# Conformer convolution and RWKV-7 block: the convolution's running sum moved from SBUF to PSUM, and the chain's four products put into one PSUM bank

## The chip, the core and the metric

The kernel runs on one core of a Trainium2 chip. Five engines share the work, each with its own queue of instructions that it takes strictly in order: PE (TensorE, matrix products; its weight loads are shown as PEld), DVE (VectorE), ACT (ScalarE), POOL (GpSimd) and SP (SyncE, which here only issues transfers). The metric is the device time of one execution in microseconds (us), with the three runs given beside it.

## What is computed

One decoder block, over 2048 tokens of 1024 channels, in float32. The parts that the change touches are the depthwise convolution and the RWKV-7 scan:

```
h = rmsnorm(x, norm_g) * (1 + scale) + shift          # adaLN from c
p = h @ w_in                                           # all branches in one projection
u = val * sigmoid(gate)
u = causal depthwise conv of u, 31 taps per channel, + conv_b
y_conv = (silu(layernorm(u)) * silu(og)) @ w_conv_out
per head, per token:                                   # 16 heads of 64
    sk    = state @ kk
    state = state * w - sk b^T + v k^T
    o     = state @ r
y_rwkv = (groupnorm(o) + bonus) * silu(r_og) @ w_rwkv_out
out = rmsnorm(x + gate * ((sigmoid(g_conv) y_conv + sigmoid(g_rwkv) y_rwkv) @ w_out), final_g)
```

## The kernel before, in words

**Tiling.** The 2048 tokens go through in 4 blocks of 512 (`TB`). Channels lie on the 128 partitions, so a tile is 128 channels by 512 tokens; 1024 channels make 8 such tiles (`KT`). Every projection is `mm3`: the float32 operands are split into a high and a low part, and three products (high-high, low-high, high-low) sum up in one PSUM tile `ps_main`. That is line 173, in the first stage 48 products of 256 columns for one tile of output.

**Two stages.** The first stage walks the 4 blocks; in each it walks 4 groups of 4 heads (`group`). Between the steps of a group it hands out `fill` work: `conv` for two channel tiles and `gates` for eight projections. Its end is at about 2690 us. The second stage (layer norm, output projections, final norm) follows; the change touches nothing in it.

**One group.** (1) `pair`, for two pairs of heads: projections, decay, and the products `As` of line 504 to 506. (2) The triangular systems of 32 by 32 are written to DRAM and read back with one system on each partition (`La`). POOL then solves them: 31 steps of a product `itmp` (line 568) and a sum `TT` (line 570), each step needing the one before. All inputs and outputs of both are in SBUF. (3) `TT` goes through DRAM back into `As`; DVE transposes 32 by 32 pieces of it (`T`, line 591), PE joins the halves (lines 597 and 606). (4) The chain: 8 chunks of 64 tokens, one after the other. In each, PE multiplies the state `S` and the older values (lines 624 and 629) into `xo`; DVE copies the half `x` of it to SBUF (`X`, line 632); PE applies the solved system (line 637); DVE scales the solution into `uv` (line 639); PE makes the state increment (line 643); DVE adds it to the state in four instructions (line 648); PE adds the solution's part to the output half `o` of `xo` (line 654), and ACT copies `o` out (line 656).

**The convolution.** `conv` makes `u` (512 tokens and 30 of the block before), and DVE sums the 31 taps: one TENSOR_SCALAR that makes `yj` (line 714) and 30 SCALAR_TENSOR_TENSOR, each `yj = u[shifted] * ck + yj` (line 717). There are 4 blocks of 8 tiles, so 960 of the latter.

**PSUM.** It has 8 banks of 2 KB per partition, and a tile takes whole banks here: `pm` 2 (`ps_main`), `pl` 1 (`late`), `px` 2 (`xo`), `pg` 1 (`gd`), `pa` 2 (`aux`). `gd` holds a chunk's solution and its state increment.

**What sets the order.** Each engine's order is written when the program is built: a scheduler places the instructions by their dependencies, its own durations and a few priorities. What another engine or a transfer must have finished is a semaphore wait in front of an instruction, and whatever is behind it in that engine's queue waits too. Accesses of two engines to one PSUM bank of one tile are kept apart by such waits, even where they touch different columns.

Of the kernel before, what the change touches and what calls it, by code (L numbers as in the profile page):

```python
# [9 lines left out]
F32 = mybir.dt.float32  # L10
# [3 lines left out]
ALU = mybir.AluOpType  # L14
AX = mybir.AxisListType
PSUM = bass.MemoryType.PSUM
DRAM = bass.MemoryType.DRAM

P = 128
D = 1024  # L20
KT = D // P
TB = 512
NTT = TB // P
# [3 lines left out]
HALO = CONVW - 1  # L27
# [55 lines left out]
def hybrid_block(ctx: ExitStack, tc: tile.TileContext, x, vecs, convk, w2a2, final_g, ada, w_in, w_co, w_ro, w_o, crow, out,  # L83
                 seq=2048, groups=(0, 1, 2, 3), phase2=True, dbg=None):
    nc = tc.nc
# [24 lines left out]
    def vc(name, j=None):  # L110
        o, w = VOFF[name]
        return v[:, o:o + w] if j is None else v[:, o + j:o + j + 1]
# [105 lines left out]
    lt = late.enter_context(tc.tile_pool(name="lt", bufs=2))  # L218
    pl = late.enter_context(tc.tile_pool(name="pl", bufs=1, space=PSUM))
    px = late.enter_context(tc.tile_pool(name="px", bufs=PXB, space=PSUM))  # L220
    pg = late.enter_context(tc.tile_pool(name="pg", bufs=1, space=PSUM))
    e1 = early.enter_context(tc.tile_pool(name="e1", bufs=1, side="right"))
    xp = early.enter_context(tc.tile_pool(name="xp", bufs=HXB, side="right"))
    hp = early.enter_context(tc.tile_pool(name="hp", bufs=1, side="right"))
# [117 lines left out]
    def hprep0(xs, ada_steps):  # L342
# [16 lines left out]
        wf_ = {}  # L359
        for k in range(KT):  # L360
            next(ada_steps)
            pt = (pl, pg)[k % 2].tile([P, NTT, P], F32, name="ps_x", tag=("late", "gd")[k % 2])
            for tt in range(NTT):
                nc.tensor.matmul(pt[:, tt, :], xs[tt][:, k * P:(k + 1) * P], dg[:, tt, :], start=(tt == 0),
                                 stop=(tt == NTT - 1), skip_group_check=True)
            hf = hx("hf0")
            nc.scalar.activation(hf, flat(pt), AF.Identity, scale=g_col[:, k:k + 1], bias=shift_col[:, k:k + 1])
            hsplit(h, k, hf)
            for i, ti in enumerate(tiles_):
                if k == i // 2:  # L370
                    hl = None
                    if i >= 2:
                        hl = [l3.tile([P, KT, P], F32R, name="w_f", tag="tk", bufs=TKB) for _ in range(4 - i)]
                        if i == 3:
                            hl.append(lt.tile([P, KT, P], F32R, name="w_f", tag="La", bufs=1))
                    wf_[ti] = load_w("in", ti, hl)
                    front[ti] = (pm, px)[i // 2].tile([P, TB], F32, name="ps_f", tag=("main", "xo")[i // 2])

            for i, ti in enumerate(tiles_):
                if ti in wf_ and k > i // 2:  # L380
                    for kk in range(0 if k == i // 2 + 1 else k - 1, k):
                        mm3k(front[ti], wf_[ti], h, kk)
# [152 lines left out]
    def group(b, g, h, lora, fill):  # L535
# [79 lines left out]
        for c in range(NCH):  # L615
# [3 lines left out]
            Se = lt.tile([P, 2, P], F32, name="Se", tag="Se", bufs=1)  # L619
            for q in range(2):  # L620
                nc.scalar.mul(Se[:, q, :], Sg[:, q, :], R[q]["pe"][:, c:c + 1])
            xo = px.tile([P, 2, P], F32, name="xo", tag="xo")
            for q in range(2):
                nc.tensor.matmul(xo[:, q, :], R[q]["KR"][:, cc, es], Sg[:, q, :], start=(q == 0), stop=False,
                                 skip_group_check=True)
# [3 lines left out]
                    nc.tensor.matmul(xo[pr_, q, hs], As[q][vr, hh, c, kcol(e)], uv[vr, c, q, hs],  # L629
                                     start=False, stop=False, skip_group_check=True)  # L630
            X = lt.tile([P, 2, P], F32, name="X", tag="X", bufs=1)
            nc.vector.tensor_copy(X[pr_], xo[pr_])  # L632
            gd = pg.tile([P, 4, P], F32, name="gd", tag="gd")
            for q in range(2):
                for hh in range(2):
                    hs = slice(64 * hh, 64 * hh + 64)
                    nc.tensor.matmul(gd[pr_, q, hs], As[q][pr_, hh, c, kcol(e)], X[pr_, q, hs],  # L637
                                     start=(q == 0 and hh == 0), stop=(q == 1 and hh == 1), skip_group_check=True)
            nc.vector.tensor_tensor(out=uv[pr_, c].rearrange("p q (h n) -> p q h n", n=64),
                                    in0=gd[pr_, 0:2].rearrange("p q (h n) -> p q h n", n=64),  # L640
                                    in1=rn[pr_, :, cc, :].unsqueeze(3).broadcast_to([64, 2, 2, 64]), op=ALU.mult)
            for q in range(2):
                nc.tensor.matmul(gd[:, 2 + q, :], R[q]["tk"][:, c, :], uv[:, c, q, :], start=(q == 0), stop=(q == 1),  # L643
                                 skip_group_check=True)
            for q in range(2):
                for hh in range(2):
                    hs = slice(64 * hh, 64 * hh + 64)
                    nc.vector.scalar_tensor_tensor(out=Sg[hs, q, hs], in0=gd[hs, 2 + q, hs],  # L648
                                                   scalar=R[q]["pe"][hs, c:c + 1], in1=Se[hs, q, hs],
                                                   op0=ALU.mult, op1=ALU.add)  # L650
            for q in range(2):
                for hh in range(2):
                    hs = slice(64 * hh, 64 * hh + 64)
                    nc.tensor.matmul(xo[vr, q, hs], As[q][:, hh, c, rcol(e)], uv[:, c, q, hs],  # L654
                                     start=False, stop=(q == 1 and hh == 1), skip_group_check=True)
            nc.scalar.copy(O[vr, cc], xo[vr])  # L656


        O16 = O.rearrange("p a q (h n) -> p a (q h) n", n=64)
# [43 lines left out]
    def conv(b, h, j):  # L703
# [6 lines left out]
        with tc.high_priority(HP):  # L710
            nc.vector.scalar_tensor_tensor(out=u[:, HALO:], in0=th, scalar=1.0, in1=pvl, op0=ALU.add, op1=ALU.mult)
        nc.gpsimd.tensor_copy(tail[:, j, :], u[:, TB:])
        yj = e2.tile([P, TB], F32, name="yj", tag="yj", bufs=1)
        nc.vector.tensor_scalar(out=yj, in0=u[:, HALO:], scalar1=ck[:, j, HALO:HALO + 1], scalar2=vc("conv_b", j),
                                op0=ALU.mult, op1=ALU.add)
        for i in range(HALO):
            nc.vector.scalar_tensor_tensor(out=yj, in0=u[:, i:i + TB], scalar=ck[:, j, i:i + 1], in1=yj,  # L717
                                           op0=ALU.mult, op1=ALU.add)
        nc.sync.dma_start(y_dram[b][j], yj)

    def gates(b, h, j, which="1234"):
# [368 lines left out]
```

## Time and profile before

| | |
|---|---|
| median of 3 runs | 3379.35 us (3379.3 to 3392.31) |
| the profiled execution, its own time | 3373.04 us |
| its span, first to last instruction | 3371.3 us |
| mean granted clock of TensorE | 0.959 |
| busy: PE, DVE, ACT, POOL | 3110.2, 2378.0, 1063.8, 1587.6 us |
| the 960 taps on DVE (line 717) | 802.3 us |
| the solve on POOL (lines 568 and 570) | 274.2 and 279.5 us |

The profile is of one execution. A view by groups has the line, the engine, the operation, output<-inputs by the program's names, shapes and the count; behind the bar the busy time in us and the mean ns of one; behind the second bar the idle time of the engine just before them, and what ended it. A view by stretches has, for each stretch of the span in us, the busy time of each engine with the number of its instructions, the granted clock of TensorE, and the share and rate of the transfers. Some products (those of line 624, for one) are recorded twice in the profile and stand once in the order.

### The profile page before, as it was taken

What the parts mean: (1) busy time and instruction counts of PE and PEld (TensorE: products, weight loads), DVE (VectorE), ACT (ScalarE), POOL (GpSimd) and SP (SyncE); (2) the same over time, 40 slices, a digit from 0 to 9 for tenths busy, and PEclk for the clock granted to TensorE, in tenths of its full rate; (3) what the DMA queues carried; (4) which work ended last, traced back from release to release, by engine and by line L of the source; (5) the groups of instructions that cost most, each with busy time, mean ns of one, the idle gap of its engine ahead of it and who ended that gap; (6) DMA issues with size and microseconds to landing.
All of it is one profiled execution on the core that took longest, in us unless ns stands there. A gap on an engine that the chain in (4) does not pass through costs nothing.

```text
span 3371.3 us, 65315 instructions
## 1 busy us (share of the span) xinstructions
PE 3110.2 (92%) x25664; PEld 2874.4 (85%) x25664; DVE 2378.0 (71%) x4712; ACT 1063.8 (32%) x1900; POOL 1587.6 (47%) x2158
## 2 busy tenths in 40 slices
PE   6889898999999989999999899999989898878998
PEld 5789898888899988898989898989989877667887
DVE  7786777776677665767666567757688656889755
ACT  4432433332223131323232314132322223344422
POOL 3375454534544535253636355727576413746201
PEclk9999999999999999899999999999999999898999
DMA  7765656663546465445554556646446655655543
GB/s 295 243 210 181 230 174 222 222 197 119 177 142 190 140 184 166 148 132 174 159 155 150 182 165 215 211 124 186 158 127 200 217 181 188 216 184 177 179 158 124
DMA packets 328468, 606.98 MB, mean 180 GB/s; under 512 B 130848, under 2 KB 147552, under 8 KB 328160
## 3 DMA queue, kind: packets, MB, share of 16 engines
q1 hardware_dynamic: 265088, 373.14, 33.7%
q0 software_dynamic: 63072, 229.67, 22.0%
q8 instruction: 202, 3.31, 0.4%
q14 instruction: 106, 0.87, 0.1%
HBM read 439.03 MB, written 162.53 MB: 178 GB/s over the span
## 4 chain that ended last, share of the span: by engine, by line
PE 46%; DVE 18%; POOL 15%; DMA 11%; issue 6%; SPq 2%; ACT 2%; POOLq 0%; DVEq 0%; ACTq 0%
PE ps_main L173 30%; POOL TT L570 5%; POOL itmp L568 5%; DVE yj L717 5%; PE aux L504 3%; DMA As<-dT 2%; DMA dT<-TT 2%; DMA La<-dA 1%; PE gd L637 1%; PE xo L654 1%; PE xo L629 1%; DMA dA<-As 1%; POOL w_lo L158 1%; PE gd L643 1%; PE pout L1007 1%
## 5 line engine op out<-in xcount | busy, mean ns | idle before, releaser
L173 PE MATMUL ps_main<-h_hi,w_hi 128*128 128x256 f32 x4608 | 981.0, 290 | 39.8 <-DVE th L700 18.0
L173 PE MATMUL ps_main<-h_hi,w_lo 128*128 128x256 f32 x4608 | 973.5, 289 | 26.4 <-POOL w_lo L158 24.4
L173 PE MATMUL ps_main<-h_lo,w_hi 128*128 128x256 f32 x4608 | 964.9, 288 | 0.2 <-DVE h_lo L328 0.2
L717 DVE SCALAR_TENSOR_TENSOR yj<-u,ck,yj 128x512 f32<-128x512 f32 x960 | 802.3, 836 | 21.8
L173 PEld LDWEIGHTS ps_main<-h_hi,w_hi 128*128 128x128 f32 x4608 | 732.0, 193 | 60.4 <-issue 21.5
L173 PEld LDWEIGHTS ps_main<-h_hi,w_lo 128*128 128x128 f32 x4608 | 730.7, 193 | 40.5 <-POOL w_lo L158 27.0
L173 PEld LDWEIGHTS ps_main<-h_lo,w_hi 128*128 128x128 f32 x4608 | 730.1, 193 | 8.2 <-issue 1.2
L568 POOL TENSOR_TENSOR itmp<-La,TT 128x126 f32<-128x126 f32 (+22 forms) x496 | 274.2, 553 | 105.1 <-DMA La<-dA 73.5
L156 ACT CAST w_hi<-w_st 128x1024 fp32r<-128x1024 f32 x167 | 175.5, 1051 | 446.5 <-DMA w_st<-w_in_t 114.7
L570 POOL TENSOR_TENSOR TT<-TT,itmp 128x126 f32<-128x126 f32 (+22 forms) x496 | 279.5, 564 | 32.7
L149 POOL DMA_DIRECT2D w_hi<-kh_in x219 | 126.8, 579 | 348.5 <-PE ps_main L173 323.9
L158 DVE TENSOR_TENSOR w_lo<-w_st,w_hi 128x1024 fp32r<-128x1024 f32 x120 | 162.9, 1357 | 132.8 <-PE ps_main L173 50.3
L648 DVE SCALAR_TENSOR_TENSOR S<-gd,pe,Se 64x64 f32<-64x64 f32 x512 | 144.7, 283 | 91.6 <-PE gd L643 82.6
L158 POOL TENSOR_TENSOR w_lo<-w_st,w_hi 128x1024 fp32r<-128x1024 f32 x47 | 117.8, 2506 | 94.8 <-ACT w_hi L156 91.2
L656 ACT COPY uv<-xo 64x256 f32<-64x256 f32 x128 | 47.1, 368 | 342.6 <-PE xo L654 270.4
L506 DVE TENSOR_TENSOR As<-aux,maskA 128x512 f32<-128x512 f32 x128 | 88.3, 691 | 86.1 <-PE aux L504 85.8
L1018 POOL TENSOR_TENSOR xt<-xt,tg 128x256 f32<-128x256 f32 x60 | 52.8, 901 | 199.2 <-DVE tg L1014 192.0
L522 POOL TENSOR_TENSOR vv<-rk,vv 128x512 f32<-128x512 f32 x32 | 45.2, 1412 | 210.6 <-PE aux L519 152.5
L504 PE MATMUL aux<-KR,BKz 128*128 128x128 f32 x1024 | 138.2, 279 | 3.1 <-ACT rk L492 2.3
L504 PEld LDWEIGHTS aux<-KR,BKz 128*128 128x128 f32 x1024 | 125.2, 191 | 7.3 <-ACT rk L492 2.8
L591 DVE STREAM_TRANSPOSE T<-As 32x32 f32<-32x32 f32 x512 | 58.0, 166 | 102.7 <-DMA As<-dT 101.5
L632 DVE COPY X<-xo 64x256 f32<-64x256 f32 x128 | 53.7, 420 | 102.8 <-PE xo L629 101.5
(293 smaller groups left out, 5867.1 us busy)
## 6 DMA issues: line engine op xcount, KB each, us to landing
w_hi<-kh_in POOLq DMA_DIRECT2D x219, 512.0 KB, 4.0
w_lo<-kl_in POOLq DMA_DIRECT2D x219, 512.0 KB, 5.1
w_st<-w_in_t SPq DMA_DIRECT2D x73, 512.0 KB, 4.6
kh_in<-w_hi SPq DMA_DIRECT2D x71, 512.0 KB, 3.1
kl_in<-w_lo SPq DMA_DIRECT2D x71, 512.0 KB, 3.9
w_st<-w_ro_t SPq DMA_DIRECT2D x32, 512.0 KB, 4.0
w_st<-w_co_t SPq DMA_DIRECT2D x32, 512.0 KB, 3.8
w_st<-w_o_t SPq DMA_DIRECT2D x32, 512.0 KB, 3.6
```

What stands on the lines that cost most here:

```text
L149: nc.gpsimd.dma_start(hi, back[0])
L156: nc.scalar.copy(hi, st)
L158: lo_eng.tensor_tensor(out=lo, in0=st, in1=hi.bitcast(F32), op=ALU.subtract)
L173: nc.tensor.matmul(ps[:, qs], ww[:, k, :], aa[k][:, qs], start=(k == 0 and t == 0 and q == 0), stop=(k == KT - 1 and t == 2 and q == ms - ...
L504: nc.tensor.matmul(pA[:, c // 2, es], BKz[:, hh, cc, es], KR[:, cc, es], start=(c == 0), stop=(c == 3), skip_group_check=True)
L506: nc.vector.tensor_tensor(out=Asb[:, hh, c4 * 4:c4 * 4 + 4, :].rearrange("p (a e) n -> p a (e n)", e=2), in0=pA, in1=flat(maskA).unsqueeze ...
L568: nc.gpsimd.tensor_tensor(out=tmp[:, :ni, :nt], in0=La[:, j:j + 1, j + 1:].broadcast_to([P, ni, nt]), in1=TT[:, :ni, j:j + 1].broadcast_to ...
L570: nc.gpsimd.tensor_tensor(out=TT[:, :ni, j + 1:], in0=TT[:, :ni, j + 1:], in1=tmp[:, :ni, :nt], op=ALU.add)
L591: nc.vector.transpose(T11[lo_, q, hh, c, :], As[q][lo_, hh, 2 * c + e, lo_])
L632: nc.vector.tensor_copy(X[pr_], xo[pr_])
L648: nc.vector.scalar_tensor_tensor(out=Sg[hs, q, hs], in0=gd[hs, 2 + q, hs], scalar=R[q]["pe"][hs, c:c + 1], in1=Se[hs, q, hs], op0=ALU.mult ...
L717: nc.vector.scalar_tensor_tensor(out=yj, in0=u[:, i:i + TB], scalar=ck[:, j, i:i + 1], in1=yj, op0=ALU.mult, op1=ALU.add)
```

## The change

Three edits, which belong together because PSUM has no ninth bank.

1. The taps. The running sum is a PSUM tile `acc` (pool `pc`, one bank). The first instruction and 29 of the 30 taps write `acc`; the last tap reads `acc` and writes `yj` in SBUF, from where it is stored as before.
2. The chain. `gd` and its pool are gone. `xo` has four parts of 128 columns instead of two: the solution goes over `x` in the first two, the state increment into the other two. Its first product no longer begins an accumulation of its own, since the bank was begun by the chunk's first product.
3. `hprep0`, which used the banks of `late` and `gd` in turn before the first block, uses those of `late` and `acc`.

```diff
--- before.py
+++ after.py
@@ -218,7 +218,7 @@
     lt = late.enter_context(tc.tile_pool(name="lt", bufs=2))
     pl = late.enter_context(tc.tile_pool(name="pl", bufs=1, space=PSUM))
     px = late.enter_context(tc.tile_pool(name="px", bufs=PXB, space=PSUM))
-    pg = late.enter_context(tc.tile_pool(name="pg", bufs=1, space=PSUM))
+    pc = late.enter_context(tc.tile_pool(name="pc", bufs=1, space=PSUM))
     e1 = early.enter_context(tc.tile_pool(name="e1", bufs=1, side="right"))
     xp = early.enter_context(tc.tile_pool(name="xp", bufs=HXB, side="right"))
     hp = early.enter_context(tc.tile_pool(name="hp", bufs=1, side="right"))
@@ -359,7 +359,7 @@
         wf_ = {}
         for k in range(KT):
             next(ada_steps)
-            pt = (pl, pg)[k % 2].tile([P, NTT, P], F32, name="ps_x", tag=("late", "gd")[k % 2])
+            pt = (pl, pc)[k % 2].tile([P, NTT, P], F32, name="ps_x", tag=("late", "acc")[k % 2])
             for tt in range(NTT):
                 nc.tensor.matmul(pt[:, tt, :], xs[tt][:, k * P:(k + 1) * P], dg[:, tt, :], start=(tt == 0),
                                  stop=(tt == NTT - 1), skip_group_check=True)
@@ -619,7 +619,9 @@
             Se = lt.tile([P, 2, P], F32, name="Se", tag="Se", bufs=1)
             for q in range(2):
                 nc.scalar.mul(Se[:, q, :], Sg[:, q, :], R[q]["pe"][:, c:c + 1])
-            xo = px.tile([P, 2, P], F32, name="xo", tag="xo")
+
+
+            xo = px.tile([P, 4, P], F32, name="xo", tag="xo")
             for q in range(2):
                 nc.tensor.matmul(xo[:, q, :], R[q]["KR"][:, cc, es], Sg[:, q, :], start=(q == 0), stop=False,
                                  skip_group_check=True)
@@ -629,23 +631,22 @@
                     nc.tensor.matmul(xo[pr_, q, hs], As[q][vr, hh, c, kcol(e)], uv[vr, c, q, hs],
                                      start=False, stop=False, skip_group_check=True)
             X = lt.tile([P, 2, P], F32, name="X", tag="X", bufs=1)
-            nc.vector.tensor_copy(X[pr_], xo[pr_])
-            gd = pg.tile([P, 4, P], F32, name="gd", tag="gd")
+            nc.vector.tensor_copy(X[pr_], xo[pr_, 0:2])
             for q in range(2):
                 for hh in range(2):
                     hs = slice(64 * hh, 64 * hh + 64)
-                    nc.tensor.matmul(gd[pr_, q, hs], As[q][pr_, hh, c, kcol(e)], X[pr_, q, hs],
+                    nc.tensor.matmul(xo[pr_, q, hs], As[q][pr_, hh, c, kcol(e)], X[pr_, q, hs],
                                      start=(q == 0 and hh == 0), stop=(q == 1 and hh == 1), skip_group_check=True)
             nc.vector.tensor_tensor(out=uv[pr_, c].rearrange("p q (h n) -> p q h n", n=64),
-                                    in0=gd[pr_, 0:2].rearrange("p q (h n) -> p q h n", n=64),
+                                    in0=xo[pr_, 0:2].rearrange("p q (h n) -> p q h n", n=64),
                                     in1=rn[pr_, :, cc, :].unsqueeze(3).broadcast_to([64, 2, 2, 64]), op=ALU.mult)
             for q in range(2):
-                nc.tensor.matmul(gd[:, 2 + q, :], R[q]["tk"][:, c, :], uv[:, c, q, :], start=(q == 0), stop=(q == 1),
+                nc.tensor.matmul(xo[:, 2 + q, :], R[q]["tk"][:, c, :], uv[:, c, q, :], start=False, stop=(q == 1),
                                  skip_group_check=True)
             for q in range(2):
                 for hh in range(2):
                     hs = slice(64 * hh, 64 * hh + 64)
-                    nc.vector.scalar_tensor_tensor(out=Sg[hs, q, hs], in0=gd[hs, 2 + q, hs],
+                    nc.vector.scalar_tensor_tensor(out=Sg[hs, q, hs], in0=xo[hs, 2 + q, hs],
                                                    scalar=R[q]["pe"][hs, c:c + 1], in1=Se[hs, q, hs],
                                                    op0=ALU.mult, op1=ALU.add)
             for q in range(2):
@@ -653,7 +654,7 @@
                     hs = slice(64 * hh, 64 * hh + 64)
                     nc.tensor.matmul(xo[vr, q, hs], As[q][:, hh, c, rcol(e)], uv[:, c, q, hs],
                                      start=False, stop=(q == 1 and hh == 1), skip_group_check=True)
-            nc.scalar.copy(O[vr, cc], xo[vr])
+            nc.scalar.copy(O[vr, cc], xo[vr, 0:2])
 
 
         O16 = O.rearrange("p a q (h n) -> p a (q h) n", n=64)
@@ -711,11 +712,12 @@
             nc.vector.scalar_tensor_tensor(out=u[:, HALO:], in0=th, scalar=1.0, in1=pvl, op0=ALU.add, op1=ALU.mult)
         nc.gpsimd.tensor_copy(tail[:, j, :], u[:, TB:])
         yj = e2.tile([P, TB], F32, name="yj", tag="yj", bufs=1)
-        nc.vector.tensor_scalar(out=yj, in0=u[:, HALO:], scalar1=ck[:, j, HALO:HALO + 1], scalar2=vc("conv_b", j),
+        acc = pc.tile([P, TB], F32, name="acc", tag="acc")
+        nc.vector.tensor_scalar(out=acc, in0=u[:, HALO:], scalar1=ck[:, j, HALO:HALO + 1], scalar2=vc("conv_b", j),
                                 op0=ALU.mult, op1=ALU.add)
         for i in range(HALO):
-            nc.vector.scalar_tensor_tensor(out=yj, in0=u[:, i:i + TB], scalar=ck[:, j, i:i + 1], in1=yj,
-                                           op0=ALU.mult, op1=ALU.add)
+            nc.vector.scalar_tensor_tensor(out=acc if i + 1 < HALO else yj, in0=u[:, i:i + TB],
+                                           scalar=ck[:, j, i:i + 1], in1=acc, op0=ALU.mult, op1=ALU.add)
         nc.sync.dma_start(y_dram[b][j], yj)
 
     def gates(b, h, j, which="1234"):
```

The number of instructions on each engine is the same before and after. The scheduler orders them anew, and the order differs in many places. Three of them follow, each before and after.

PE, the step from one chunk of the chain to the next, in the first group of the third block. `tk` and `uv` make the state increment, `S` and `KR` are the operands of the next chunk's first products; numbers at the end of a name are buffers. Before:

```order
L643 MATMUL gd<-uv,tk 128x128 [waits DVE_49]
L643 MATMUL gd<-uv,tk 128x128
L654 MATMUL xo<-uv,As 64x64 x4
L173 MATMUL ps_main<-h_hi,w_lo 128x256
L173 MATMUL ps_main<-h_hi,w_hi 128x256 x2
```

After, the same products, of which the increment (now line 644) stands 18 rows earlier:

```order
L626 MATMUL xo<-S_417,KR 128x128 [waits DVE_49,Activation_49]
L173 MATMUL ps_main<-h_lo,w_hi 128x256
L655 MATMUL xo<-uv,As 64x64 [waits DVE_49]
L655 MATMUL xo<-uv,As 64x64 x3
L626 MATMUL xo<-S_417,KR 128x128
L631 MATMUL xo<-uv,As 64x64 x4
```

The product into `o` (line 654, now 655) no longer follows the increment: it waits for DVE, whose state update reads the same bank, and stands between the first products of the next chunk.

POOL, the middle of the solve of the third block's second group (`w_hi<-kh_in` and `w_lo<-kl_in` are reloads of weights, `uv<-uv,gst` is the group norm of the group before). Before:

```order
L568 TENSOR_TENSOR itmp<-La,TT 128x8x16 [waits Pool_49]
L570 TENSOR_TENSOR TT<-TT,itmp 128x8x16 [waits Pool_49]
L671 TENSOR_TENSOR uv<-uv,gst 128x4x256 [waits DVE_49,Activation_49]
L149 DMA w_hi<-kh_in_4310 128x1024 [waits DMASW4_49,PE_49]
L568 TENSOR_TENSOR itmp<-La,TT 128x9x15 [waits Pool_49]
```

After:

```order
L568 TENSOR_TENSOR itmp<-La,TT 128x8x16 [waits Pool_49]
L570 TENSOR_TENSOR TT<-TT,itmp 128x8x16 [waits Pool_49]
L149 DMA w_hi<-kh_in_4297 128x1024 [waits DMASW4_49,PE_49]
L568 TENSOR_TENSOR itmp<-La,TT 128x9x15 [waits Pool_49]
L150 DMA w_lo<-kl_in_4298 128x1024 [waits DMASW5_49,PE_49]
```

The group norm's two instructions (lines 671 and 678) stood inside the solve of six of the 16 groups, and now stand inside none.

DVE, the end of the solve of the second block's third group (`T<-As` is the first instruction that needs the solve's result). Before:

```order
L711 SCALAR_TENSOR_TENSOR u<-th,ps_main 128x512 [waits PE_49,Activation_49]
L714 TENSOR_SCALAR yj<-u,ck,v 128x512 [waits DMAHW3_49,DVE_49]
L717 SCALAR_TENSOR_TENSOR yj<-u,ck,yj 128x512 [waits DVE_49] x2
L632 COPY X<-xo 64x256 [waits PE_49]
L717 SCALAR_TENSOR_TENSOR yj<-u,ck,yj 128x512 [waits DVE_49] x3
L591 STREAM_TRANSPOSE T_13214<-As 32x32 [waits DMAHW6_49]
```

After:

```order
L719 SCALAR_TENSOR_TENSOR yj<-u,ck,acc 128x512 [waits DMAHW3_49,DVE_49]
L649 SCALAR_TENSOR_TENSOR S_419<-xo,pe,Se 64x64 [waits PE_49]
L649 SCALAR_TENSOR_TENSOR S_419<-xo,pe,Se 64x64 x3
L634 COPY X<-xo 64x256 [waits PE_49]
L591 STREAM_TRANSPOSE T_13178<-As 32x32 [waits DMAHW6_49]
```

The first `T` stands behind fewer taps. Counted over the 16 groups, 692 taps stood between the last instruction on `As` before the solve and the first `T`, and 615 do after the change.

## The prediction

> **What bounds the kernel now.** I read four views in this order: the stretches of the first stage, the waits, the timeline at one solve, and the groups of DVE and POOL.
>
> ```profile
> 1008.00:1176.00 168.00, 168.00 (x1547) 159.14 (x1546) 114.59 (x259) 47.68 (x94) 83.50 (x152) 1.00 0.55 164
> sum 2520.00, PE 2377.41 PEld 2235.93 DVE 1782.08 ACT 744.60 POOL 1292.36; mean PE 594.35 PEld 558.98 DVE 445.52 ACT 186.15 POOL 323.09
> 168.00:822.00 654.00, 597.08 (x5223) 561.01 (x5222) 482.67 (x923) 222.78 (x372) 331.31 (x396) 0.94 0.58 195
> 822.00:1478.00 656.00, 627.21 (x5683) 590.65 (x5682) 445.44 (x997) 188.13 (x364) 297.06 (x503) 0.97 0.53 160
> 1478.00:2138.00 660.00, 633.56 (x5738) 596.29 (x5737) 447.33 (x987) 187.21 (x358) 333.10 (x527) 0.97 0.57 174
> 2138.00:2688.00 550.00, 519.56 (x4604) 487.97 (x4604) 406.64 (x819) 146.48 (x263) 330.89 (x489) 0.97 0.56 172
> ```
>
> The first row is PE at its best: never idle, clock 1.00, 168.00 us for 1547 products, 108.6 ns each. The other four are the four blocks after the start, and the sum is theirs. At that pace their 21,248 products need 2307 us; they took 2520. Of the 213 us lost PE was idle for 143 (2520 less 2377) and 70 went into a slower pace at a granted clock of 0.94 to 0.97. So PE bounds this stage, 8% above its own floor, and nothing in the change makes its work smaller: it can win only from those 213 us. In the rows here an idle microsecond comes with 70/143 = 0.49 us of slower pace; I use 1.49 for each idle microsecond won.
>
> Where does PE lose it? Much of it right behind the solves. These are the first, the worst and the best of 16 stretches of 24 us, each from the end of a solve on, and the sum of all 16:
>
> ```profile
> 225.00:249.00 24.00, 20.74 (x229) 18.87 (x227) 23.44 (x64) 6.42 (x12) 10.64 (x11) 1.00 0.63 189
> 1181.00:1205.00 24.00, 14.84 (x113) 14.09 (x112) 10.97 (x47) 3.34 (x7) 4.98 (x11) 0.79 0.53 132
> 1023.00:1047.00 24.00, 24.00 (x211) 23.23 (x211) 20.89 (x61) 5.99 (x13) 7.71 (x13) 1.00 0.64 176
> sum 384.00, PE 323.43 PEld 298.90 DVE 267.60 ACT 77.67 POOL 116.77; mean PE 20.21 PEld 18.68 DVE 16.72 ACT 4.85 POOL 7.30
> ```
>
> In a seventh of the stage, 384 us, lie 61 of its 143 idle microseconds. The worst one shows how, in the timeline of DVE and PE:
>
> ```profile
> 1178.47 2.31 DVE L717 SCALAR_TENSOR_TENSOR yj<-u,ck,yj 128x512 f32<-128x512 f32 x3
> 1189.17 0.96 DVE L591 STREAM_TRANSPOSE T<-As 32x32 f32<-32x32 f32 x8 [8.39 <-DMA As<-dT]
> 1194.77 0.48 DVE L591 STREAM_TRANSPOSE T<-As 32x32 f32<-32x32 f32 x4 [4.63 <-DMA As<-dT]
> 1195.18 0.37 DVE L639 TENSOR_TENSOR uv<-gd,rn 64x256 f32<-64x256 f32 x1
> 1195.60 0.80 PE L643 MATMUL gd<-uv,tk 128*128 128x128 f32 x2 [9.16 <-DVE uv L639]
> ```
>
> DVE runs out of taps, stands at `T` until the solve's result is back from DRAM, and `uv` of the chain stands behind `T`; PE waits 9.16 us for `uv`. The solve is late, and everything behind it in two queues is late with it. Over the whole run:
>
> ```profile
> DVE T L591 <- DMA As<-dT: 101.5, 35, 8.4
> PE gd L643 <- DVE uv L639: 24.9, 7, 9.2
> PE late L597 <- DVE T L591: 15.9, 9, 3.3
> PE ps_main L173 <- DVE th L700: 18.0, 5, 10.4
> PE ps_main L173 <- DVE carry L401: 9.1, 8, 1.9
> PE gd L637 <- DVE X L632: 6.7, 6, 2.9
> PE xo L624 <- DVE S L648: 6.4, 5, 3.8
> ```
>
> **Why the solve is late.** Its steps on POOL in two solves, beside DVE:
>
> ```profile
> 1145.29 2.34 DVE L717 SCALAR_TENSOR_TENSOR yj<-u,ck,yj 128x512 f32<-128x512 f32 x3
> 1145.55 0.70 POOL L568 TENSOR_TENSOR itmp<-La,TT 128x96 f32<-128x96 f32 x1
> 1147.15 0.72 POOL L568 TENSOR_TENSOR itmp<-La,TT 128x115 f32<-128x115 f32 x1
> 1147.95 0.43 POOL L570 TENSOR_TENSOR TT<-TT,itmp 128x115 f32<-128x115 f32 x1
> 1016.04 0.39 POOL L570 TENSOR_TENSOR TT<-TT,itmp 128x96 f32<-128x96 f32 x1
> 1137.76 0.69 DVE L700 SCALAR_TENSOR_TENSOR th<-th,ps_main 128x512 f32<-128x512 f32 x1 [0.45 <-ACT th L698]
> 1137.97 0.24 POOL L570 TENSOR_TENSOR TT<-TT,itmp 128x30 f32<-128x30 f32 x1
> 1178.40 0.93 POOL L570 TENSOR_TENSOR TT<-TT,itmp 128x30 f32<-128x30 f32 x1
> ```
>
> Beside taps a step of 115 elements takes 0.72 us; its twin of the same size, begun when the taps had ended at 1147.63, takes 0.43. With 30 elements it is 0.93 beside taps and 0.24 under `th`, an instruction of the tap's kind and size that has one input in PSUM. So what slows POOL is a DVE instruction with two inputs in SBUF, and one with an input in PSUM does not.
>
> **The change part by part.** The groups that price it:
>
> ```profile
> L717 DVE SCALAR_TENSOR_TENSOR yj<-u,ck,yj 128x512 f32<-128x512 f32 x960 | 802.3, 836 | 21.8
> L717 DVE SCALAR_TENSOR_TENSOR yj<-u,ck,yj x960: 695/752/2862, 152.3 to 2665.1; 128x512 f32<-128x512 f32 x192
> L397 DVE SCALAR_TENSOR_TENSOR vv<-ps_main,v,t 128x511 f32<-128x511 f32 x31 | 23.1, 746 | 40.9 <-ACT t L395 40.6
> L568 POOL TENSOR_TENSOR itmp<-La,TT 128x126 f32<-128x126 f32 (+22 forms) x496 | 274.2, 553 | 105.1 <-DMA La<-dA 73.5
> L570 POOL TENSOR_TENSOR TT<-TT,itmp 128x126 f32<-128x126 f32 (+22 forms) x496 | 279.5, 564 | 32.7
> L714 DVE TENSOR_SCALAR yj<-u,ck,v 128x512 f32<-128x512 f32 x32 | 20.7, 648 | 14.6 <-DMA y_d<-yj 13.7
> L953 DVE TENSOR_SCALAR ve<-pvar x3: 680/682/684, 2923.4 to 3119.3; 128x512 f32<-128x512 f32 x3
> L648 DVE SCALAR_TENSOR_TENSOR S<-gd,pe,Se 64x64 f32<-64x64 f32 x512 | 144.7, 283 | 91.6 <-PE gd L643 82.6
> ```
>
> *The solve.* Its 62 steps take (274.2+279.5)/16 = 34.6 us. Undisturbed rows go from 0.24 us (30 elements) to 0.43 (115); I take 0.39 for all, 24 us: 10 us less per solve. DVE waits at `T` for 101.5/16 = 6.3 us per solve, and PE is idle 61/16 = 3.8 in the stretch behind it, so 10 us cover both. I don't take the whole 61 (weights are missing in some of these stretches too) but the two waits that hang on `T`: 24.9 + 15.9 = 41 us of PE, and with the slower pace 61. What is late next is the reload of weights, below.
>
> *The taps.* Undisturbed one takes 752 ns (the median), and a tap-like instruction with a tensor in PSUM and a scalar per partition 746 (`vv`): reading PSUM costs nothing. No engine but PE writes PSUM in this trace, so the write has no price. From below: 695 ns, the shortest tap. From above: one more fixed part. The 64-column `S` takes 283 ns, a 512-column tap 752, so a column costs 1.05 ns and the fixed part is 216; 752 + 216 = 968. I take 752, since the read had no extra price. That is 84 ns or 81 us of DVE less in all, a tenth of the taps; a tenth of what PE waits for DVE's queue (18.0 + 9.1 + 6.7 + 6.4) is 4 us, with pace 6. At 968 it is 127 us more on DVE, which is idle for 738 of the stage's 2520 us: the 38 taps that stand before a `T` in the mean (615/16) make 5.0 us more, within the 6.3 that DVE waits there. This cover ends at 836 + 6300/38 = 1002 ns a tap.
>
> [...]
>
> *The first instruction* of a convolution writes PSUM: `ve`, the same operation with PSUM at one end, takes 682 against 648: 1 us in all, under DVE's idle time. *The store of* `yj` held the next convolution's first instruction for 13.7 us; now only its last tap can wait. Nothing on PE hangs on it.
>
> *The chain's bank.* The product into `o` waits for all four state updates and stands in PE's queue before the second of the next chunk's first products, at 112 steps between chunks. It costs nothing as long as PE reaches it after the updates. The order leaves as much other work between the increment and that place as before, where PE waited for `S` 6.4 us in all, 5 times. From above: the updates of the second pair, 2 x 283 ns, less one product, 0.45 us each time, 50 us, with pace 75. I take 0.
>
> *The order.* Six solves lose the group norm that stood inside them. `T` stands behind 615 instead of 692 taps, 77 x 0.836 = 64 us earlier on DVE, which a solve 160 us shorter in all allows.
>
> Sum: 61 + 6 = 67 us. Span 3371.3 − 67 = 3304; the execution's own time lies 1.7 above it (3373.04), 3306. The median of the runs is 6.3 above the profiled execution (3379.35), so I predict **3312 us**.
>
> **The rivals.** *Hidden: the reloads of weights take the solve's place.* POOL's queue also issues the weight reloads, which wait until PE has used up a buffer, and they stand inside the solves:
>
> ```profile
> POOL w_hi L149 <- PE ps_main L173: 323.9, 90, 12.7
> PE ps_main L173 <- POOL w_lo L158: 24.4, 13, 4.6
> ```
>
> For it: 323.9 us of POOL's waiting, and a reload that waits for PE holds the next step of the solve. Against: it's 90 waits for 219 reloads, while POOL in the solves had no idle time to give. If it keeps two thirds of the gain: 67/3 = 22, 3379 − 22 = 3357.
>
> *Slower: taps still disturb POOL.* If writing PSUM, or the tap's one SBUF input, holds POOL as before, solves last as long and `T`, 64 us earlier in DVE's order, blocks DVE that much longer, with `uv`, `X` and `th` behind it. PE paid 61 idle for DVE's 101.5, so 38, with pace 57: 3379 + 57 = 3436. It decides where a step beside taps stays above 0.6 us. Against it: 0.24 us under `th`, which has one input in PSUM but writes SBUF; so it keeps 10%.
>
> [...]
>
> *The bank holds the chain.* At the upper price of 75 it eats the gain: 3312 + 75 = 3387, no change. It decides where PE comes to the product into `o` before the last update has ended; for it stands the order, against it the 6.4 us.
>
> *Slow taps*, well above 1002 ns: at two more fixed parts, 1184, 38 taps end 13.2 us later, 6.9 beyond DVE's wait; 16 x 6.9 = 110, with pace 165: 3544.
>
> **How the numbers follow.** This measurement tells about 0.5% (17 us) from no change: 3362 to 3396. Forecast 60%, with a range of its own of 3275 to 3345; hidden reloads 18%, half of it beyond 3362; the bank 8%; disturbed POOL 10%; slow taps 4%. Faster 0.60 + 0.10 = 0.70; same 0.08 + 0.08 = 0.16; slower 0.14. The range takes in reloads and bank, leaves out both slower cases and a little below: 3255 to 3392. Its low end is all 61 idle us behind the solves with pace (91), the 40 us for DVE with half of it won, 30.
>
> **What would show it.** Right: steps of lines 568 and 570 near 370 ns in the mean and a solve's 62 near 24 us; `T` waiting under 40 us in all; PE idle in the stage near 100 us; taps near 750 with no long tail. Wrong: steps still above 500 ns; a wait of PE at the product into `o` (line 655) of tens of us; taps above 1 us; or `T` not waiting while PE's idle time is as before, with weights as the releaser.

## The result and the profile after

The changed kernel takes 3264.79 us (median of 4 runs, 3256.74 to 3270.96), the kernel before 3382.87 (4 runs, 3379.3 to 3392.31). The ratio is 0.9645, with a 95% interval of 0.9615 to 0.9676. The profiled execution went from 3373.04 to 3256.74 us and its span from 3371.3 to 3255.0: 116 us less, where the prediction's sum had 67.

The blocks of the first stage after the start, in the view by stretches of the changed kernel. They hold 21,292 products here (21,248 before) and end at 2572 us instead of 2688:

```profile
168.00:754.00 586.00, 565.01 (x5121) 533.50 (x5121) 442.27 (x917) 220.42 (x371) 276.19 (x394) 0.97 0.65 216
754.00:1384.00 630.00, 618.31 (x5636) 583.90 (x5635) 435.40 (x985) 186.07 (x358) 255.33 (x502) 0.98 0.56 167
1384.00:2028.00 644.00, 630.36 (x5746) 595.76 (x5745) 448.24 (x985) 186.40 (x358) 281.89 (x523) 0.98 0.60 179
2028.00:2572.00 544.00, 523.62 (x4789) 493.97 (x4788) 392.20 (x842) 149.28 (x271) 278.09 (x493) 0.97 0.58 176
sum 2404.00, PE 2337.30 PEld 2207.13 DVE 1718.11 ACT 742.18 POOL 1091.50; mean PE 584.32 PEld 551.78 DVE 429.53 ACT 185.54 POOL 272.88
```

All 116 us lie here: 2404 us against 2520. PE is idle for 67 us (2404 less 2337) where it was for 143, so 76 of the 116 are idle time won. At the prediction's 108.6 ns a product the work needs 2312 us, so 25 go into a slower pace where 70 did: 45 more. The 44 additional products in these stretches take 5 back. The first block gave most: 586 us instead of 654, with 102 products fewer; the second 630 instead of 656, the third 644 instead of 660, the fourth 544 instead of 550 with 185 products more.

The groups of POOL and DVE that the prediction priced, by line, engine, operation and tile, with busy time and mean:

```profile
L719 DVE SCALAR_TENSOR_TENSOR acc<-u,ck,acc 128x512 f32<-128x512 f32 x928 | 697.6, 752 | 22.6
L719 DVE SCALAR_TENSOR_TENSOR yj<-u,ck,acc 128x512 f32<-128x512 f32 x32 | 23.8, 743 | 0.6
L716 DVE TENSOR_SCALAR acc<-u,ck,v 128x512 f32<-128x512 f32 x32 | 25.8, 806 | 0.9
L568 POOL TENSOR_TENSOR itmp<-La,TT 128x126 f32<-128x126 f32 (+22 forms) x496 | 179.7, 362 | 99.7 <-DMA La<-dA 66.9
L570 POOL TENSOR_TENSOR TT<-TT,itmp 128x126 f32<-128x126 f32 (+22 forms) x496 | 189.4, 382 | 33.4
```

A step of the solve went from 553 and 564 ns to 362 and 382; the 62 steps of one solve take (179.7 + 189.4)/16 = 23.1 us instead of 34.6. The tap is at its undisturbed 752 ns. Its row by tile shows that the long tail is gone too; the maximum was 2862:

```profile
L719 DVE SCALAR_TENSOR_TENSOR acc<-u,ck,acc x928: 698/756/758, 153.5 to 2511.7; 128x512 f32<-128x512 f32 x186
```

Beside taps a step now costs what it cost without them. From the timeline of DVE and POOL in the last block:

```profile
2363.93 3.11 DVE L719 SCALAR_TENSOR_TENSOR acc<-u,ck,acc 128x512 f32<-128x512 f32 x4
2365.35 0.39 POOL L570 TENSOR_TENSOR TT<-TT,itmp 128x96 f32<-128x96 f32 x1
```

The step of 96 elements takes 0.39 us under four taps in a row. Before, a step of this size took 0.39 where no tap ran beside it, and 0.70 beside taps. Counted over the 992 steps of the 16 solves in each trace, those that had taps beside them for more than half of their time took 0.70 us in the mean before and 0.38 after; those with none took 0.36 and 0.34.

The waits of the whole run, in us, times, longest:

```profile
DVE T L591 <- DMA As<-dT: 31.8, 24, 4.6
PE aux L249 <- ACT rh L490: 35.2, 10, 11.6
PE xo L626 <- DVE S L649: 5.4, 5, 2.1
PE ps_main L173 <- DVE carry L401: 4.1, 4, 1.8
PE ps_main L173 <- POOL w_lo L158: 2.7, 3, 1.5
PE ps_main L173 <- DVE th L701: 2.5, 1, 2.5
PE xo L638 <- DVE X L634: 1.3, 2, 0.9
PE xo L644 <- DVE uv L640: 0.3, 1, 0.3
POOL w_hi L149 <- PE ps_main L173: 546.5, 155, 12.6
```

Two rows of the kernel before, to go with them:

```profile
PE aux L249 <- ACT rh L490: 12.4, 6, 6.6
PE late L683 <- POOL uv L678: 9.8, 6, 5.8
```

DVE's wait at `T` fell from 101.5 to 31.8 us. PE's wait for `uv` fell from 24.9 to 0.3, and its waits for `T` (15.9) and for the group norm's `uv` (line 678, 9.8) have no row any more. But waits far from the solve fell as well: `w_lo` from 24.4 to 2.7, `th` from 18.0 to 2.5, `X` from 6.7 to 1.3, `carry` from 9.1 to 4.1. PE's wait for `rh`, in the preparation of a pair, grew from 12.4 to 35.2. POOL's wait for PE at the reloads of weights grew from 323.9 to 546.5. There is no row for the product into `o` (line 655).

### The profile page after: what moved, and what is told of

The parts are those of the page before. It is cut to its first block, busy times and chain, and to the rows that moved or that the text cites. A ratio compares the mean times of both kernels' runs of the same rounds, so it can differ in the third digit from the quotient of the medians.

```text
span 3255.0 us, 65241 instructions
## 1 busy us (share of the span) xinstructions
PE 3069.2 (94%) x25664; PEld 2844.5 (87%) x25664; DVE 2309.0 (71%) x4712; ACT 1060.8 (33%) x1900; POOL 1386.8 (43%) x2158
## 3 DMA queue, kind: packets, MB, share of 16 engines
q1 hardware_dynamic: 265088, 373.14, 35.2%
## 5 line engine op out<-in xcount | busy, mean ns | idle before, releaser
L173 PE MATMUL ps_main<-h_hi,w_hi 128*128 128x256 f32 x4608 | 965.0, 287 | 8.7 <-DVE carry L401 4.1
L173 PEld LDWEIGHTS ps_main<-h_hi,w_hi 128*128 128x128 f32 x4608 | 722.2, 191 | 23.2 <-DVE carry L401 5.0
L173 PEld LDWEIGHTS ps_main<-h_hi,w_lo 128*128 128x128 f32 x4608 | 721.6, 190 | 13.8 <-POOL w_lo L158 3.9
L719 DVE SCALAR_TENSOR_TENSOR acc<-u,ck,acc 128x512 f32<-128x512 f32 x928 | 697.6, 752 | 22.6
L149 POOL DMA_DIRECT2D w_hi<-kh_in x219 | 126.1, 576 | 572.1 <-PE ps_main L173 546.5
L568 POOL TENSOR_TENSOR itmp<-La,TT 128x126 f32<-128x126 f32 (+22 forms) x496 | 179.7, 362 | 99.7 <-DMA La<-dA 66.9
L649 DVE SCALAR_TENSOR_TENSOR S<-xo,pe,Se 64x64 f32<-64x64 f32 x512 | 144.8, 283 | 100.9 <-PE xo L644 91.5
L570 POOL TENSOR_TENSOR TT<-TT,itmp 128x126 f32<-128x126 f32 (+22 forms) x496 | 189.4, 382 | 33.4
L621 ACT ACTIVATE Se<-S,pe 128x128 f32<-128x128 f32 x256 | 89.1, 395 | 349.5 <-DVE S L649 349.4
L640 DVE TENSOR_TENSOR uv<-xo,rn 64x256 f32<-64x256 f32 x128 | 53.8, 420 | 112.0 <-PE xo L638 111.0
L634 DVE COPY X<-xo 64x256 f32<-64x256 f32 x128 | 54.0, 422 | 108.6 <-PE xo L631 107.2
L150 POOL DMA_DIRECT2D w_lo<-kl_in x219 | 120.1, 549 | 14.3 <-PE ps_main L173 8.0
```

The source lines that it names most:

```text
L149: nc.gpsimd.dma_start(hi, back[0])
L150: nc.gpsimd.dma_start(lo, back[1])
L173: nc.tensor.matmul(ps[:, qs], ww[:, k, :], aa[k][:, qs], start=(k == 0 and t == 0 and q == 0), stop=(k == KT - 1 and t == 2 and q == ms - ...
L568: nc.gpsimd.tensor_tensor(out=tmp[:, :ni, :nt], in0=La[:, j:j + 1, j + 1:].broadcast_to([P, ni, nt]), in1=TT[:, :ni, j:j + 1].broadcast_to ...
L570: nc.gpsimd.tensor_tensor(out=TT[:, :ni, j + 1:], in0=TT[:, :ni, j + 1:], in1=tmp[:, :ni, :nt], op=ALU.add)
L649: nc.vector.scalar_tensor_tensor(out=Sg[hs, q, hs], in0=xo[hs, 2 + q, hs], scalar=R[q]["pe"][hs, c:c + 1], in1=Se[hs, q, hs], op0=ALU.mult ...
```

## The experiments

Each ratio is to the kernel before on the same chip, with its 95% interval. Diffs are against the changed kernel, except where said.

Each of these kernels was ordered anew, and the orders differ in many places: on DVE, the kernel with two SBUF inputs parts from the changed one after 231 of 4712 instructions. How much a new order can shift in a place that the taps do not reach is seen at one product of the second stage (`ps_main<-m_hi,w_hi`). PE waits there 6.8 us in the kernel before and 19.4 in the changed one, and 10.2 and 23.4 in the two kernels with the reloads in SP's queue. Half a per cent between two of these kernels therefore shows no cause.

### The taps back in SBUF, all else as changed

```diff
-        acc = pc.tile([P, TB], F32, name="acc", tag="acc")
-        nc.vector.tensor_scalar(out=acc, in0=u[:, HALO:], ...
+        nc.vector.tensor_scalar(out=yj, in0=u[:, HALO:], ...
-            nc.vector.scalar_tensor_tensor(out=acc if i + 1 < HALO else yj, in0=u[:, i:i + TB],
-                                           scalar=ck[:, j, i:i + 1], in1=acc, ...
+            nc.vector.scalar_tensor_tensor(out=yj, in0=u[:, i:i + TB],
+                                           scalar=ck[:, j, i:i + 1], in1=yj, ...
```

> The changed kernel with the taps back in SBUF; the chain keeps its one bank per chunk. Theory A (taps with two inputs in SBUF hold up POOL's solve): the steps of the solve are back at a mean of 540 to 570 ns (362 and 382 in the changed kernel), a solve's 62 at 33 to 35 us, and the time is that of the kernel before within 1% (3350 to 3415 us). Theory B (the gain is the new order, or the bank): most of the 118 us stay, under 3310 us. Theory C (DVE's own time): the taps are back at a mean of 836 ns, and the time with them; C and A agree here.

Measured: 3382.08 us, ratio 0.9973 [0.9951, 0.9995]. Groups and waits of this kernel:

```profile
L570 POOL TENSOR_TENSOR TT<-TT,itmp 128x126 f32<-128x126 f32 (+22 forms) x496 | 271.4, 547 | 33.9
DVE T L591 <- DMA As<-dT: 94.5, 28, 7.9
PE ps_main L173 <- POOL w_lo L158: 25.1, 9, 4.7
PE xo L655 <- DVE S L649: 7.1, 4, 3.1
PE aux L249 <- ACT rh L490: 45.1, 13, 17.1
```

The steps are slow again, the waits of before are back (`w_lo` at 25.1), and the gain is gone but for 0.3%. So the shared bank and the order that comes with it neither win nor lose much in sum; nearly all of the 3.5% comes from the taps. PE's wait at the product into `o`, the price that the prediction gave the shared bank, is 7.1 us here and has no row in the changed kernel. PE's wait for `rh` is 45.1 us here, with the taps in SBUF, where it was 12.4 in the kernel before. Its growth therefore belongs to the new order or the bank, and not to the taps.

### Taps in PSUM, but with two inputs in SBUF

```diff
-                                           scalar=ck[:, j, i:i + 1], in1=acc, op0=ALU.mult, op1=ALU.add)
+                                           scalar=ck[:, j, i:i + 1], in1=u[:, HALO:], op0=ALU.mult, op1=ALU.add)
```

> The taps write PSUM as in the changed kernel, but their third input is the unshifted u in SBUF instead of the running sum (so what is computed is not the convolution). Two inputs are in SBUF again, and the order is built with the same durations as in the changed kernel. Theory A: steps of the solve at 520 to 580 ns, and 3330 to 3400 us, since the order does not allow for it. Theory B: under 3300 us, as the order is near that of the changed kernel. If it is the write to SBUF that disturbs POOL, steps stay under 400 ns and the time under 3290.

Measured: 3401.67 us, ratio 1.0044 [1.0026, 1.0062].

```profile
L719 DVE SCALAR_TENSOR_TENSOR acc<-u,ck 128x512 f32<-128x512 f32 x928 | 796.8, 859 | 20.2
L570 POOL TENSOR_TENSOR TT<-TT,itmp 128x126 f32<-128x126 f32 (+22 forms) x496 | 273.4, 551 | 34.3
DVE T L591 <- DMA As<-dT: 101.7, 31, 7.9
PE xo L638 <- DVE X L634: 36.6, 9, 7.8
PE ps_main L173 <- POOL w_lo L158: 24.7, 13, 4.7
PE ps_main L173 <- DVE th L701: 1.8, 2, 1.5
```

Writing PSUM by itself wins nothing: with the second input in SBUF again, steps are at 551 ns, taps at 859 and the wait at `T` at 101.7 us. PE waits for `X` and `w_lo` as before or longer, but not for `th`. The time lies 2 us above theory A's range.

### Taps that read PSUM and write SBUF

```diff
-            nc.vector.scalar_tensor_tensor(out=acc if i + 1 < HALO else yj, in0=u[:, i:i + TB],
+            nc.vector.scalar_tensor_tensor(out=yj, in0=u[:, i:i + TB],
```

> The taps read the bank in PSUM but write SBUF (the sum is not carried on, so what is computed is not the convolution). Theory A: one input in SBUF is enough, steps of the solve at 360 to 400 ns, 3245 to 3290 us. If it is the write into SBUF that disturbs POOL: steps above 500 ns, above 3330 us.

Measured: 3249.92 us, ratio 0.9597 [0.9573, 0.9621].

```profile
L719 DVE SCALAR_TENSOR_TENSOR yj<-u,ck,acc 128x512 f32<-128x512 f32 x960 | 713.9, 744 | 31.0 <-DMA y_d<-yj 8.1
L570 POOL TENSOR_TENSOR TT<-TT,itmp 128x126 f32<-128x126 f32 (+22 forms) x496 | 188.5, 380 | 33.4
```

The whole gain is here. With the run before it this settles what the change does: it takes the second SBUF input away from 960 instructions. Where they write makes no difference beyond the 0.5% by which this kernel lies below the changed one (0.9597 against 0.9645); that half per cent is not explained, and the order is another one.

### DVE's own time

Four copies of `acc` onto itself in each convolution, 128 in all:

```diff
+            if i % 7 == 6:
+                nc.vector.tensor_copy(acc, acc)
```

> The changed kernel with four copies of the running sum onto itself in each convolution, 128 in all, some 0.7 us each: 90 us more for DVE, as much as its taps lost to disturbance before the change, but known to the scheduler. Theory C (it is DVE's own time that was won): 3330 us or more. Theory S or R (it is the delays that the order does not allow for): 3260 to 3290 us.

Measured: 3259.34 us, ratio 0.9618 [0.9598, 0.9638].

```profile
L722 DVE COPY acc<-acc 128x512 f32<-128x512 f32 x128 | 89.0, 695 | 2.9
PE ps_main L173 <- POOL w_lo L158: 5.2, 6, 1.6
PE ps_main L173 <- DVE carry L401: 11.2, 10, 2.2
```

89 us more on DVE, more than the 81 that the taps lost, cost nothing that can be measured. So DVE has that much time to spare where the order knows of it, and its busy time alone is not what was won. The taps' loss before was of another kind: 66 of these 81 us lay in 49 taps of more than 1.2 us, each of them beside a GpSimd instruction of more than 1.2 us. This run cannot show that such delays cost nothing; the kernel with odd convolutions, below, suggests that they cost something.

### The solve made longer, and the order made with it

```diff
             nc.gpsimd.tensor_tensor(out=tmp[:, :ni, :nt], in0=La[:, j:j + 1, j + 1:]...
+            nc.gpsimd.tensor_tensor(out=tmp[:, :ni, :nt], in0=La[:, j:j + 1, j + 1:]...
```

> The changed kernel with each product of the solve issued twice, so a solve's steps take 22.6 + 11.2 = 34 us undisturbed, as long as before the change, but known to the scheduler. Theory A1 (the length of the solve is what costs, whoever causes it): at least half of the gain is given back, 3325 us or more. Theory A2 (what costs is that the disturbed steps are longer than the order allows for): the order puts other work there, 3265 to 3295 us, with DVE waiting at T under 45 us in all.

Measured: 3294.46 us, ratio 0.9725 [0.9697, 0.9753].

```profile
L570 POOL TENSOR_TENSOR itmp<-La,TT 128x126 f32<-128x126 f32 (+22 forms) x496 | 182.2, 367 | 33.1
DVE T L593 <- DMA As<-dT: 42.7, 28, 8.8
```

Each solve has 11 us of work more ((180.6 + 182.2 + 188.5)/16 = 34.5 us, with the other two groups of this kernel), as much as before the change. From its first step to its last it lasts 66 us in the mean of the 16, by the start of the first and the end of the last of its instructions in the trace; in the kernel before it lasted 51, in the changed one 41. Yet only 0.8% of the 3.5% goes, and `T` waits 42.7 us, as theory A2 had it. A long solve by itself is therefore not what cost 118 us. The extra products were known when the order was written. That the slowing by taps is in no order, and that this difference is the reason, is an inference: no run has the same delay once known and once unknown.

### Where the second input costs: even or odd convolutions

In the order, `conv` of even `j` mostly lies beside the solves, and of odd `j` beside the rest of a group.

```diff
-                                           scalar=ck[:, j, i:i + 1], in1=acc, op0=ALU.mult, op1=ALU.add)
+                                           scalar=ck[:, j, i:i + 1], in1=acc if j % 2 else u[:, HALO:], op0=ALU.mult, op1=ALU.add)
```

and in the other kernel `in1=u[:, HALO:] if j % 2 else acc`.

> As the run with two SBUF inputs, but only in the convolutions of even channel tiles (their sum is not the convolution's). In the changed kernel's profile nearly all taps that run during a solve are of an even tile, those of odd tiles run beside the other work of a group. Theory S (the loss is in the solves): steps of the solve at 510 to 570 ns, and most of the 137 us between that run and the changed kernel come back, 3350 to 3395 us. Theory R (the loss is shared with the rest: taps that wait for POOL's long instructions, and those for taps): about half, 3305 to 3340 us.

> The other half: two SBUF inputs only in the convolutions of odd channel tiles (their sum is not the convolution's). Theory S: steps of the solve near 380 ns, 3255 to 3290 us. Theory R: steps near 380 ns and all the same 3305 to 3340 us, with some taps of 2 us and more that wait for POOL.

Measured: even 3340.22 us, ratio 0.9864 [0.9841, 0.9886]; odd 3298.13 us, ratio 0.9739 [0.9713, 0.9764]. Of the kernel with even ones:

```profile
L570 POOL TENSOR_TENSOR TT<-TT,itmp 128x126 f32<-128x126 f32 (+22 forms) x496 | 260.3, 525 | 33.1
DVE T L591 <- DMA As<-dT: 70.1, 33, 5.3
PE ps_main L173 <- POOL w_lo L158: 23.6, 9, 5.9
```

And with odd ones:

```profile
L570 POOL TENSOR_TENSOR TT<-TT,itmp 128x126 f32<-128x126 f32 (+22 forms) x496 | 197.6, 398 | 33.5
DVE T L591 <- DMA As<-dT: 35.9, 23, 5.3
PE ps_main L173 <- POOL w_lo L158: 10.1, 7, 3.3
```

The kernel with even ones has taps of both kinds in one order, and so holds the sharpest comparison. The solve's steps with an even tap beside them for more than half of their time took 0.71 us in the mean (437 steps), those with an odd tap 0.33 (83 steps).

All taps with two SBUF inputs cost 4.0% against the changed kernel (1.0044 less 0.9645), the even half 2.2%, the odd half 0.9%; the rest, 0.9%, appears only with both. The split is rough, since each kernel has its own order and the intervals are 0.2 to 0.3% to either side. So most of it goes with the convolutions beside the solves, as theory S had it, but not all: with odd ones the solve is nearly undisturbed and `T` waits 35.9 us, little more than the changed kernel's 31.8, and still 0.9% is lost. There the long taps are back, as theory R said: 38 of more than 1.2 us, the longest 2.78, 51 us more than as many undisturbed ones. Neither theory's figures were met in full: the even kernel lies at the top of R's range, the odd one between the two ranges. PE's wait for `w_lo`, which I had set apart from the solve, comes back in full with the even ones (23.6 us), and in part with the odd ones (10.1).

### The reloads of weights in SP's queue

The rival of the prediction that POOL's queue is held by the reloads can be tried by issuing them elsewhere:

```diff
-            nc.gpsimd.dma_start(hi, back[0])
-            nc.gpsimd.dma_start(lo, back[1])
+            nc.sync.dma_start(hi.bitcast(F32), back[0].bitcast(F32))
+            nc.sync.dma_start(lo.bitcast(F32), back[1].bitcast(F32))
```

> The changed kernel with the 438 reloads of weights issued from SP's queue in place of POOL's. POOL in the changed kernel waits 546 us at them for PE, the solve's steps behind them. If that wait still costs: solves end some us sooner, DVE's 32 us at T shrink, 3235 to 3255 us. If the solve is early enough by now: no change, 3255 to 3275. If SP's queue, which waits for much else, brings weights late: above 3290 us.

Measured, with the taps in PSUM: 3230.45 us, ratio 0.9538 [0.9519, 0.9557]. This beats both kernels: 34 us, about 1.1%, below the changed one.

```profile
SPq L149 <- PE ps_main L173: 866.1, 171, 30.1
L570 POOL TENSOR_TENSOR TT<-TT,itmp 128x126 f32<-128x126 f32 (+22 forms) x496 | 187.0, 377 | 37.2
DVE T L591 <- DMA As<-dT: 40.5, 38, 3.4
PE aux L249 <- ACT rh L490: 23.5, 6, 9.2
```

The wait for PE has moved to SP's queue. The steps are as long as in the changed kernel (377 ns), but a solve now lasts 31 us from first to last step instead of 41. Of these 10 us, 4.9 are POOL's time for issuing the reloads and 4.4 its idle time (9.3 us in a solve of the changed kernel, 4.9 here). The expectation that `T` would wait less was wrong: its wait grew from 31.8 to 40.5 us, while the wait for `rh` shrank from 35.2 to 23.5.

The same edit in the kernel before, with the taps in SBUF:

> The kernel before, with nothing changed but the queue: the reloads of weights (lines 149 and 150) are issued by SP instead of POOL. Taps keep two SBUF inputs. Theory L (the taps stretch the solve's steps, and POOL waiting for PE at a reload is a second cost of its own): the steps stay above 500 ns, the solve loses only its reload waits, and the time falls by about what the same edit gained in the changed kernel, 34 us of 3265, so to about 3350 us (ratio 0.985 to 0.995). Theory M (either of the two is enough: the loss is that the solve is late, and the reload waits inside it make it late as well): without them the solve ends early enough in spite of slow steps, T waits under 40 us, and most of the 118 us is won: below 3300 us (ratio below 0.976). Theory N (the reload waits only show once the steps are fast, since before they fell into time that POOL spends on the solve anyway): no change, ratio 0.995 to 1.005.

Measured: 3389.59 us (10 runs), ratio 1.0002 [0.9983, 1.0021].

```profile
L570 POOL TENSOR_TENSOR TT<-TT,itmp 128x126 f32<-128x126 f32 (+22 forms) x496 | 281.1, 567 | 36.8
DVE T L591 <- DMA As<-dT: 102.4, 30, 12.7
PE late L683 <- POOL uv L678: 36.3, 7, 9.5
PE gd L643 <- DVE uv L639: 11.7, 3, 5.9
```

Nothing is won, as theory N had it. A solve lasts 44 us in the mean instead of 51, but 5.6 of these 7 us are the issuing: POOL's idle time in a solve was 4.7 us before and is 4.3 here, so the solve had hardly waited at reloads. `T` still waits 102.4 us. In this order PE's waits for the chain's `uv` and for `T` fell by 26 us (40.8 to 14.8), and its wait for the group norm's `uv` grew by as much, from 9.8 to 36.3. Moving the reloads wins nothing before the change and 1.1% after it; in that sense they are the next limit behind the one that was taken away. That the slow steps alone kept the shorter solve from paying is not shown, since the order is another one.

## Why the prediction was right or wrong

The direction and the mechanism were right; the gain was 118 us where 67 were forecast, and the 3264.79 us lie in the lower part of the range, below the forecast's own 3275 to 3345. The low end had been worked out from 61 + 20 = 81 us of idle time won, and 76 were, but partly in other waits than it named. (Its two terms, 91 and 30, give 3258, not 3255.) By its steps:

- *The solve's steps.* Forecast 0.39 us each and 24 us for 62; measured 0.372 and 23.1. The argument from `th`, an instruction of the tap's kind with one input in PSUM, held, also for the write to PSUM that no row before showed.
- *The waits that hang on `T`.* Forecast 41 us of PE; 24.9 + 15.9 less 0.3 = 40.5 measured.
- *What DVE's faster queue gives PE: the term that was mis-sized.* I took a tenth of PE's waits for DVE's queue, 4 us (6 with pace), and nothing of PE's wait for `w_lo`. In the rows `th`, `w_lo`, `X`, `carry` and `S` together fell by 48.6 us (64.6 to 16.0). The reasoning was that a tap a tenth shorter shortens these waits by a tenth. The runs show more than one cause. `w_lo` and `X` follow the second SBUF input: `w_lo` waits 23.6 to 25.1 us in the kernels that have it in all or the even convolutions, and 2.7 and 5.2 in the changed kernel and in the one with DVE's 89 us more; `X` waits 6.7 to 36.6 us in the former, and 1.3 and 2.7 in the latter. So these two, 27 of the 48.6 us, were the same disturbance seen in another place, and I had counted only the waits with `T` or the chain's `uv` in their row. `th` and `carry`, 20.5 us, do not follow it: `th` waits 1.8 us with all taps at two SBUF inputs, and `carry` 11.2 with none. Why they fell stays open; each order has its own. Against all this PE's wait for `rh` grew by 22.8 us, which I had not foreseen and which came with the bank or the order. In the four blocks alone the five waits fell by 44.7 us (53.7 to 9.0) and the group norm's `uv` by 9.8. Sum: 40.5 + 44.7 + 9.8 − 22.8 = 72 of the 76 us of idle time won.
- *The pace.* Forecast 0.49 us per idle microsecond; 45 with 76, or 0.59. Why PE's pace is slower where it idles more stays open; the granted clock of the blocks rose from 0.94 to 0.97 up to 0.97 to 0.98.
- *The taps.* 752 forecast, 752 measured in the mean. The last tap of each convolution, which reads the sum from PSUM and writes SBUF, took 743, and the median with everything in SBUF was 752; so the trace shows no price for the sum read from PSUM.
- *The first instruction* was forecast at 682 ns and took 806: 5 us instead of 1, on an engine whose time was free.
- *The chain's bank.* Forecast 0, with an upper price of 75; no row for it in the changed kernel. *The order*, not priced: together with the bank it is worth 0.3% (0.05 to 0.5) in the first run.
- *Hidden reloads.* The rival had the mechanism and not the price: with 34 us still to be had at the reloads, the change kept 118 of 152 us, not the third that I gave it. Its argument against, that POOL had no idle time to give in the solves, was about right for the kernel before: 4.7 us in a solve, against 9.3 after. Its row of 323.9 us spoke for it, and moving the reloads won nothing before; with the row at 546.5 it won 34 us. The row alone did not tell.
- *Disturbed POOL, slow taps*: the rows exclude both (362 and 382 ns; no tap above 758). The first is the kernel with two SBUF inputs, which the rival put at 3436; that run took 3401.67.

## What to carry to other kernels

In this kernel the VectorE taps with two SBUF inputs lengthened a chain of short GpSimd instructions beside them from 0.37 to 0.56 us a step in the mean, and took 836 ns themselves in the mean, where their median was 752. One input in PSUM ended both, wherever the result was written: steps at 0.37 us, and taps at 752 ns with the sum in PSUM and 744 with the result in SBUF. Where another kernel has such a pair, the same move is worth a trial. As the upper price of such a change take every wait of the bounding engine that hangs on either queue, not only those with the slowed result in their row; here such rows held 115 us of the kernel before, and 76 us of idle time were won. When it is done, ask what holds the freed queue next: moving the reloads was worth nothing before and 1.1% after.

## What the runs showed of the hardware that I had not expected

The TENSOR_SCALAR that writes PSUM from SBUF took 814 ns in the median, where the same one writing SBUF took 547. (The means, 806 and 648, hide part of this, since the longest of the 32 took 1752 before.) The SCALAR_TENSOR_TENSOR of the taps showed no price for PSUM on either side: a mean of 752 ns with the sum read there and written there, of 743 with it read there and written to SBUF, and a median of 752 with everything in SBUF. So the price of PSUM was not one number for DVE here. The convolution's first instruction before, and then after:

```profile
L714 DVE TENSOR_SCALAR yj<-u,ck,v x32: 531/547/1752, 148.0 to 2620.3; 128x512 f32<-128x512 f32 x32
L716 DVE TENSOR_SCALAR acc<-u,ck,v x32: 760/814/816, 149.4 to 2477.3; 128x512 f32<-128x512 f32 x32
```

Beside taps a long GpSimd instruction lost as much here as a step of the solve did. The group of `w_lo` (1024 elements) before, and then after:

```profile
L158 POOL TENSOR_TENSOR w_lo<-w_st,w_hi 128x1024 fp32r<-128x1024 f32 x47 | 117.8, 2506 | 94.8 <-ACT w_hi L156 91.2 <-ACT xTs L319 2.9 <-PE ps_main L173 0.5
```

```profile
L158 POOL TENSOR_TENSOR w_lo<-w_st,w_hi 128x1024 fp32r<-128x1024 f32 x47 | 113.7, 2418 | 115.0 <-ACT w_hi L156 99.1 <-PE ps_main L173 8.5 <-PE aux L430 4.1
```

The mean is only 3.5% shorter, where the solve's steps are a third shorter, because few of the 47 ran beside taps. Before the change, the 13 with taps beside them for more than half of their time took 2.72 us in the mean and the 26 with none 2.38; after it both kinds took 2.43. The 0.34 us that each lost is what a step of the solve lost too (0.70 less 0.36): nearly its own length again for the step, and a seventh for `w_lo`.

These 13 lost some 4 us together, while PE's wait for `w_lo` fell from 24.4 us to 2.7. So it fell mostly because POOL's queue came to the instruction earlier, more likely than because the instruction became faster; this is argued.
